# Global attention: row maxima by a scan, values two fifths at a time, the last product on GpSimd

## The chip, the cores and the metric

The kernel runs on one core of a Trainium2 chip. The time is that of one execution on the device, in microseconds (us). A core has five engines that run side by side, each through its own queue in order: TensorE (PE in the profile; its weight loads are PEld), VectorE (DVE), ScalarE (ACT), GpSimd (POOL) and SyncE (SP), which here only issues DMAs. Matmuls write to PSUM, which has eight banks of 128 x 512 fp32; VectorE and ScalarE read PSUM, GpSimd doesn't.

## The reference

Two layers of a diffusion block on 1024 latent tokens of width 1024, with 256 context tokens. Each layer has three groups of heads side by side (global attention, pooling, neighbourhood attention), each gated, and one output projection. The change touches the global attention alone: 8 query heads of 64 in two key groups, 1024 queries against 1280 keys (1024 latent, 256 context).

```python
def dense_attn(q, k, v):
    s = jnp.einsum("bqkgd,bskd->bkgqs", q, k).astype(jnp.float32)
    p = jax.nn.softmax(s, axis=-1).astype(v.dtype)
    o = jnp.einsum("bkgqs,bskd->bqkgd", p, v)
    return o.reshape(o.shape[0], o.shape[1], -1)
...
a_out = global_gqa(aq, ak, av, ak_c, av_c)
...
y = jnp.concatenate([a_out * silu(ag), b_out * silu(bg), n_out * silu(ng)], axis=-1) @ w_out[l]
```

## The kernel before

Each layer runs in stages: projections of the tokens, neighbourhood attention (with the context tokens' own attention in layer 0), global attention, output projection. TensorE's order is written out by hand (the order of the program's text); for the other engines a planner chooses the order from the program's dependencies and its own estimates of time, and once chosen it is fixed: an instruction that waits holds up all behind it on its engine.

Global attention is cut into eight **units**, gunits[0] to [7]: a unit is 512 queries (cc) of a pair of heads (hi = 0, 1) that share a key group g. A unit has these parts.

- **Maxima** (shift, L974). A softmax needs the row maxima before its exponentials. For each head, 8 matmuls of 128 queries x 512 keys (L985), each into a bank of its own with one reduction by VectorE (L986), then 2 banks of context keys (L990, L991). A last small reduction (L994) gives the negative maxima of 8 x 128 queries. shift_rows (L996) transposes them on TensorE, copies them, and two DMAs write them into row 0 of the second query operand q2, whose matmul (L1012) then adds the negative maximum and the low part of the product to the scores. The maxima of unit i are made while unit i - 1 runs: 21 steps in a list, which shift_step pops.
- **Scores** (L1006). They come transposed (keys down, queries across) in fifths kp = 0 to 4, 256 keys each. For a head and a fifth 4 matmuls (L1011, L1012) fill a tile of two banks, one exponential (L1014) reads it and writes a tile gp of 128 x 1024. There are two such tiles of banks (ps_w). s14 stands below for the scores of head 1, fifth 4.
- **Sums**: the tiles of a head are added up in gacc, fifths 1 to 3 by GpSimd (L1019, L1022), fifth 4 by VectorE (L1022), which also folds the two halves (L1024). Matmuls with ones add over the partitions (L1040).
- **Values** (L1026): for each 128 keys two matmuls of 64 output columns, one for each head, add into one bank, ps_c (L1031; the trace has two records for each such fp32 matmul). They run one fifth behind the scores; the last fifth and the sums are done in the next unit.
- **Finish** (L1037): the reciprocal of the sums by Ln, Exp and a step of refinement on VectorE (L1044 to L1048), the product of the output and the gate on GpSimd (L1049), the product of the two on VectorE (L1050), and store_u (L803), which writes the result as a high part hh on ScalarE (L806) and the rest hl on VectorE (L807), the operands of the output projection.

Maxima, transposes and sums take turns in three PSUM banks (ps_b, by ps_one); a bank is free again when its reader is done. The gp tiles and gacc share a ring of seven buffers in SBUF (tag prob, PB = 7). The loop over the units stands at L1117; unit 7 has no maxima to make.

## Time and profile before

| | us |
|---|---|
| median of 3 runs | 1550.68 (1550.53 to 1553.64) |
| the profiled execution | 1550.23 |
| its span, first to last instruction | 1548.5 |
| layer 0, global attention | from about 523 to 740 |
| layer 1, global attention | from about 1237 to 1454 |

The granted clock of TensorE was 0.989 in the mean. A row of the groups gives line, engine, operation, what it writes and reads, shape and count, then the busy time in us and the mean of one in ns, then the engine's idle time before it and who ended it. A row of the timeline gives start and length in us, then the instruction, and in brackets the idle time before it with its releaser. A row of the waits gives who waited for whom: us in total, times, the longest.

### The profile page before, as it was taken

The page shows a single profiled execution, that of the slowest core. Times are in us where ns is not written, and L with a number is a line of the kernel's source. Part 1 is how long each engine was busy: PE and PEld are TensorE (multiplying, and loading weights), DVE is VectorE, ACT ScalarE, POOL GpSimd, SP SyncE. Part 2 cuts the span into 40 slices and gives each one's busy share as a digit, 9 for nine tenths or more (in the row PEclk, how much of TensorE's full clock was granted, in tenths as well). Part 3 has the DMA queues.
Part 4 walks back from the last instruction along what each step waited for, and adds up shares of the span by engine and source line. Part 5 has one row for each costly group of instructions (what it writes and reads, how often), then busy time and mean ns, then how long its engine had stood idle before and what let it go on. Part 6 is the DMA issues. An engine that isn't in the chain of part 4 may idle for free.

```text
span 1548.5 us, 22305 instructions
## 1 busy us (share of the span) xinstructions
PE 1474.4 (95%) x8001; PEld 1074.7 (69%) x8001; DVE 855.6 (55%) x1721; ACT 661.8 (43%) x1296; POOL 506.0 (33%) x586
## 2 busy tenths in 40 slices
PE   5999999999899999998999999999989899999999
PEld 3787777788788555454788888878778754554577
DVE  3535234552477687875534444464357768786522
ACT  4543132333587544444322443332458544444400
POOL 0232336000132556566001132470013166565300
PEclk8999999999999999999999999999999999999999
DMA  9436455537746110101412223253696211001331
GB/s 306 148 98 219 128 157 164 165 103 191 169 123 167 45 42 21 41 7 41 176 55 104 87 79 104 76 149 83 174 218 158 79 31 41 22 21 41 120 132 55
DMA packets 153040, 167.91 MB, mean 108 GB/s; under 512 B 35384, under 2 KB 112032, under 8 KB 152864
## 3 DMA queue, kind: packets, MB, share of 16 engines
q1 hardware_dynamic: 152928, 166.48, 37.1%
q8 instruction: 63, 1.03, 0.3%
q14 instruction: 49, 0.40, 0.1%
HBM read 126.45 MB, written 40.86 MB: 108 GB/s over the span
## 4 chain that ended last, share of the span: by engine, by line
PE 52%; DVE 8%; ACT 3%; issue 2%; DMA 1%; POOL 1%; SPq 0%; DVEq 0%; ACTq 0%; POOLq 0%
PE ps_c L1031 7%; PE ps_w L1184 4%; PE ps_w L1187 4%; PE ps_w L1185 4%; PE ps_w L1011 4%; PE ps_w L1012 3%; PE ps_w L417 3%; PE ps_w L418 3%; PE ps_w L416 3%; PE ps_b L985 3%; DVE gt L1050 2%; DVE gmx L986 2%; PE ps_c L877 1%; DVE gacc L1022 1%; PE ps_w L426 1%
## 5 line engine op out<-in xcount | busy, mean ns | idle before, releaser
L1014 ACT ACTIVATE gp<-ps_w 128x1024 f32<-128x1024 f32 x160 | 162.4, 1022 | 183.5 <-PE ps_w L1012 147.2
L416 PE MATMUL ps_w<-wh,hh 128*128 128x512 f32 (+1 forms) x624 | 235.7, 378 | 1.7 <-ACT wh L285 1.7
L417 PE MATMUL ps_w<-wl,hh 128*128 128x512 f32 (+1 forms) x624 | 228.9, 367 | 0.3 <-DVE wl L286 0.2
L418 PE MATMUL ps_w<-wh,hl 128*128 128x512 f32 (+1 forms) x624 | 228.3, 366 | 0.0
L986 DVE TENSOR_REDUCE gmx<-ps_b 128x1 f32<-128x512 f32 x256 | 171.7, 685 | 75.7 <-PE ps_b L985 71.6
L1031 PE MATMUL ps_c<-gp,av 128*64 128x512 f32 x640 | 165.7, 611 | 10.4 <-ACT gp L1014 10.4
L1022 POOL TENSOR_TENSOR gacc<-gacc,gp 128x1024 f32<-128x1024 f32 x64 | 161.4, 2550 | 25.8 <-ACT gp L1014 25.5
L416 PEld LDWEIGHTS ps_w<-wh,hh 128*128 128x128 f32 x624 | 118.6, 190 | 26.8 <-issue 4.4
L418 PEld LDWEIGHTS ps_w<-wh,hl 128*128 128x128 f32 x624 | 117.9, 189 | 20.6
L417 PEld LDWEIGHTS ps_w<-wl,hh 128*128 128x128 f32 x624 | 118.1, 189 | 19.3 <-DVE wl L286 0.8
L1012 PE MATMUL ps_w<-gq,kst 128*128 128x512 f32 x320 | 126.2, 394 | 0.0
L1184 PE MATMUL ps_w<-woh,hh 128*128 128x512 f32 x272 | 109.1, 401 | 0.0
L1185 PE MATMUL ps_w<-wol,hh 128*128 128x512 f32 x272 | 107.1, 394 | 0.0
L637 DVE TENSOR_REDUCE qss<-sq 128x8 f32<-128x512 f32 (+2 forms) x58 | 31.1, 537 | 131.6 <-ACT sq L635 131.3
L1031 PEld LDWEIGHTS ps_c<-gp,av 128*64 128x64 f32 x640 | 42.7, 137 | 88.0 <-issue 65.7
L1019 POOL TENSOR_TENSOR gacc<-gp 128x1024 f32<-128x1024 f32 x32 | 75.8, 2368 | 50.7 <-ACT gp L1014 50.7
L286 DVE TENSOR_TENSOR wl<-wraw,wh 128x512 fp32r<-128x512 f32 (+1 forms) x96 | 66.5, 708 | 38.1 <-ACT wh L285 36.6
L1187 PE MATMUL ps_w<-woh,hl 128*128 128x512 f32 x272 | 85.0, 394 | 0.0
L852 ACT ACTIVATE prob<-ps_w,nm 128x768 f32<-128x768 f32 (+2 forms) x88 | 73.4, 834 | 21.9 <-DVE nm L841 16.6
L424 PE MATMUL ps_w<-hh,wh 128*128 128x512 f32 (+1 forms) x208 | 80.7, 388 | 0.9 <-ACT wh L285 0.9
L870 ACT ACTIVATE probt<-ps_b 128x512 f32<-128x512 f32 (+2 forms) x152 | 73.6, 532 | 17.1 <-PE ps_b L868 16.7
L635 ACT ACTIVATE sq<-ps_w 128x512 f32<-128x512 f32 (+2 forms) x58 | 27.9, 481 | 121.7 <-PE ps_w L418 121.7
(225 smaller groups left out, 2992.1 us busy)
## 6 DMA issues: line engine op xcount, KB each, us to landing
wmod<-in_w_mod_dram SPq DMA_DIRECT2D x48, 512.0 KB
wraw<-in_w_in_dram SPq DMA_DIRECT2D x64, 256.0 KB
gq<-qad SPq DMA_DIRECT2D x64, 128.0 KB
woraw<-in_w_out_dram SPq DMA_DIRECT2D x14, 512.0 KB
wraw<-in_w_in_dram SPq DMA_DIRECT2D x48, 128.0 KB
kst<-knd SPq DMA_DIRECT2D x16, 320.0 KB
qad<-qkhi SPq DMA_DIRECT2D x18, 256.0 KB
qad<-qklo SPq DMA_DIRECT2D x18, 256.0 KB
```

The lines of the kernel that those rows point to most:

```text
L416: PE.matmul(ps[:, :n], a, wh[:, off:off + n], start=(k == 0), stop=False)
L417: PE.matmul(ps[:, :n], a, wl[:, off:off + n], start=False, stop=False)
L418: PE.matmul(ps[:, :n], b, wh[:, off:off + n], start=False, stop=(k == KT - 1))
L424: PE.matmul(ps[:, :n], wh[:, fs], hh[:, k, ts_], start=(k == 0), stop=False)
L986: DVE.reduce_max(out=mx[:, qt, half:half + 1], in_=S, axis=AX.X)
L1012: PE.matmul(S[:, i, :], k2[:, kc], st.q2[hi], start=False, stop=True)
L1014: ACT.activation(out=p, in_=S, func=AF.Exp)
L1022: eng.tensor_tensor(out=st.acc[hi], in0=st.acc[hi], in1=pf, op=ALU.add)
L1031: PE.matmul(st.o[hi * 64:(hi + 1) * 64, :], av[:, kt, g * 64:(g + 1) * 64], st.p[hi, kp][:, i, :], start=(kt == 0), stop=(kt == NTT - 1))
L1184: PE.matmul(ps[:, i2, :], a, oh[:, cs], start=(k == 0), stop=False)
L1185: PE.matmul(ps[:, i2, :], a, ol[:, cs], start=False, stop=False)
L1187: PE.matmul(ps[:, i2, :], b, oh[:, i2 * 512:(i2 + 1) * 512], start=False, stop=(k == KT - 1))
```

## The change

- For units 2 to 7 shift2 takes the place of shift. The context keys' maxima come first, by the same reductions. Then, for each 128 queries, both banks of 512 keys are filled one after the other (a pair). ScalarE copies the first into SBUF, and one running scan of VectorE over the second bank and the copy, begun with the context maximum, keeps the maximum so far; its last element is the row maximum. A negation per two scans takes the place of the last reduction. The copies lie in the memory of the two tables of the neighbourhood attention, which become one tile each. Steps have weights now (a pair counts 2), and shift_step gives credits, so a unit still makes 21 of them.
- The values run two fifths at a time: after s02 fifths 0 and 1, after s04 fifths 2 and 3, and the last fifth in the next unit after s01. Right behind it stand the sums and the finish, which came after the third fifth before.
- The finish's last product moves to GpSimd, without its sign; the sign goes into the write of hh and the difference hl.
- gacc leaves the ring: it lies in the memory of nv (values of the neighbourhood attention) for even units and in two kst buffers for odd ones. In unit 7, head 0's additions from fifth 2 on go to VectorE.

```diff
--- before.py
+++ after.py
@@ -742,7 +742,8 @@
         akx, attx = ExitStack(), ExitStack()
         ak_ = akx.enter_context(pool(f"attk{l}", side=left))
 
-        tab_bufs = [(ak_.tile([P, 14, 64], F32, name=f"ntab{i}"), ak_.tile([P, 10, 64], F32, name=f"itab{i}")) for i in range(2)]
+        tab_mem = [ak_.tile([P, 24, 64], F32, name=f"tab{i}") for i in range(2)]
+        tab_bufs = [(t[:, 0:14], t[:, 14:24]) for t in tab_mem]
 
         def kst():
             return ak_.tile([P, NT], F32R, name="kst", bufs=6)
@@ -954,7 +955,7 @@
             return gks[g]
 
 
-        def ga_unit(cc, g, pr):
+        def ga_unit(n, cc, g, pr):
             f = 2 * g + pr
             cs = slice(cc * 512, (cc + 1) * 512)
             st = _Env()
@@ -986,12 +987,41 @@
                     DVE.reduce_max(out=mx[:, qt, half:half + 1], in_=S, axis=AX.X)
                     return
                 q0 = 2 * (j - 8)
-                for i in range(2):
-                    PE.matmul(S[:, i * 256:(i + 1) * 256], q1[:, (q0 + i) * P:(q0 + i + 1) * P], k1[:, SEQ:NT], start=True, stop=True)
-                DVE.reduce_max(out=mx[:, q0:q0 + 2, 2], in_=S.rearrange("p (a b) -> p a b", a=2), axis=AX.X)
+                shift_ctx(hi, q0, S, mx[:, q0:q0 + 2, 2])
                 if hi and j == 9:
                     st.nn = small.tile([P, 8], F32, tag="gnn", name="gnn")
                     DVE.tensor_reduce(out=st.nn, in_=st.mx.rearrange("p h q k -> p (h q) k"), op=ALU.max, axis=AX.X, negate=True)
+            def shift_ctx(hi, q0, S, out):
+                for i in range(2):
+                    PE.matmul(S[:, i * 256:(i + 1) * 256], st.q1[hi][:, (q0 + i) * P:(q0 + i + 1) * P], gk(g)[0][:, SEQ:NT],
+                              start=True, stop=True)
+                DVE.reduce_max(out=out, in_=S.rearrange("p (a b) -> p a b", a=2), axis=AX.X)
+            def shift2(i):
+                hi, j = divmod(i, 6)
+                if i == 0:
+                    load2()
+                    st.mx = small.tile([P, 8], F32, tag="gmx2", name="gmx2")
+                    st.nn = small.tile([P, 8], F32, tag="gnn", name="gnn")
+                if j < 2:
+                    c = 4 * hi + 2 * j
+                    shift_ctx(hi, 2 * j, ps_one("ps_m"), st.mx[:, c:c + 2])
+                    return
+                qt = j - 2
+                if qt % 2 == 0:
+                    st.run = tab_mem[qt // 2].rearrange("p a k -> p (a k)")[:, 0:1024].rearrange("p (a b) -> p a b", a=2)
+                S = [ps_one("ps_m") for _ in range(2)]
+                for half in range(2):
+                    PE.matmul(S[half], st.q1[hi][:, qt * P:(qt + 1) * P], gk(g)[0][:, half * 512:(half + 1) * 512], start=True, stop=True)
+                r, c = st.run[:, qt % 2], 4 * hi + qt
+                ACT.activation(out=r, in_=S[0], func=AF.Copy)
+                DVE.tensor_tensor_scan(out=r, data0=S[1], data1=r, initial=st.mx[:, c:c + 1], op0=ALU.max, op1=ALU.max)
+                if qt % 2:
+                    DVE.tensor_scalar(out=st.nn[:, c - 1:c + 1], in0=st.run[:, :, 511], scalar1=-1.0, scalar2=None, op0=ALU.mult)
 
             def shift_rows():
 
@@ -1015,10 +1045,10 @@
                 st.p[hi, kp] = p
                 pf = p.rearrange("p a b -> p (a b)")
                 if kp == 1:
-                    st.acc[hi] = ap_.tile([P, 1024], F32, name="gacc", tag="prob", bufs=PB)
+                    st.acc[hi] = accs[n % 2][hi]
                     POOL.tensor_tensor(out=st.acc[hi], in0=st.p[hi, 0].rearrange("p a b -> p (a b)"), in1=pf, op=ALU.add)
                 elif kp > 1:
-                    eng = DVE if kp == 4 else POOL
+                    eng = DVE if kp == 4 or (n == 7 and hi == 0) else POOL
                     eng.tensor_tensor(out=st.acc[hi], in0=st.acc[hi], in1=pf, op=ALU.add)
                 if kp == 4:
                     DVE.tensor_tensor(out=st.acc[hi][:, 0:512], in0=st.acc[hi][:, 0:512], in1=st.acc[hi][:, 512:1024], op=ALU.add)
@@ -1034,31 +1064,40 @@
                     st.osb = ap_.tile([P, 512], F32, name="gosb", tag="fin", bufs=4)
                     ACT.activation(out=st.osb, in_=st.o, func=AF.Copy)
 
+            def sums():
+                st.s = ps_one("ps_gs")
+                for hi in range(2):
+                    PE.matmul(st.s[hi * 64:(hi + 1) * 64, :], ones, st.acc[hi][:, 0:512], start=True, stop=True)
             def finish():
-                s_ps = ps_one("ps_gs")
-                for hi in range(2):
-                    PE.matmul(s_ps[hi * 64:(hi + 1) * 64, :], ones, st.acc[hi][:, 0:512], start=True, stop=True)
                 gt = ap_.tile([P, 512], F32, name="ggate", tag="fin", bufs=4)
                 SP.dma_start(out=gt, in_=agd[f, :, cs])
                 r0 = ap_.tile([P, 512], F32, name="gr0", tag="fin", bufs=4)
-                ACT.activation(out=r0, in_=s_ps, func=AF.Ln)
+                ACT.activation(out=r0, in_=st.s, func=AF.Ln)
                 ACT.activation(out=r0, in_=r0, func=AF.Exp, scale=-1.0)
                 t1 = ap_.tile([P, 512], F32, name="gt1", tag="fin", bufs=4)
-                DVE.tensor_tensor(out=t1, in0=s_ps, in1=r0, op=ALU.mult)
+                DVE.tensor_tensor(out=t1, in0=st.s, in1=r0, op=ALU.mult)
                 DVE.scalar_tensor_tensor(out=t1, in0=t1, scalar=-2.0, in1=r0, op0=ALU.add, op1=ALU.mult)
                 POOL.tensor_tensor(out=gt, in0=gt, in1=st.osb, op=ALU.mult)
-                DVE.scalar_tensor_tensor(out=t1, in0=t1, scalar=-1.0, in1=gt, op0=ALU.mult, op1=ALU.mult)
-                store_u(f, cc * 512, 512, t1)
-
-            return shift, scores, values, finish, load, shift_rows
-
-        gunits = [ga_unit(cc, g, pr) for cc in range(2) for g in range(2) for pr in range(2)]
+                POOL.tensor_tensor(out=gt, in0=gt, in1=t1, op=ALU.mult)
+                hi, lo = hh[:, f, cs], hl[:, f, cs]
+                ACT.activation(out=hi, in_=gt, func=AF.Identity, scale=-1.0)
+                DVE.scalar_tensor_tensor(out=lo, in0=gt, scalar=-1.0, in1=hi.bitcast(F32), op0=ALU.mult, op1=ALU.subtract)
+            return shift, scores, values, finish, load, shift_rows, shift2, sums
+        gunits = [ga_unit(4 * cc + 2 * g + pr, cc, g, pr) for cc in range(2) for g in range(2) for pr in range(2)]
 
         shifts = []
         for i, u in enumerate(gunits):
-            own = [lambda u=u, j=j: u[0](j) for j in range(20)]
-            shifts += own[:2] + ([gunits[i - 1][5]] if i else []) + own[2:]
-        shifts.append(gunits[-1][5])
+            if i < 2:
+                own = [(1, lambda u=u, j=j: u[0](j)) for j in range(20)]
+            else:
+                own = [(1 if j % 6 < 2 else 2, lambda u=u, j=j: u[6](j)) for j in range(12)]
+            shifts += own[:2] + ([(1, gunits[i - 1][5])] if i else []) + own[2:]
+        shifts.append((1, gunits[-1][5]))
         for i in range(2):
             early(len(units) - 12, gunits[i][4])
 
@@ -1077,10 +1116,16 @@
         n_shifts = 7 if last else 10
         n_ahead = 21 + GA_AHEAD
 
+        credit = [0]
         def shift_step(n, least=0):
-            for _ in range(n):
-                if len(shifts) > least:
-                    shifts.pop(0)()
+            credit[0] += n
+            while len(shifts) > least and shifts[0][0] <= credit[0]:
+                w, fn = shifts.pop(0)
+                credit[0] -= w
+                fn()
+            if len(shifts) <= least:
+                credit[0] = 0
 
         n_all = len(shifts)
         for n, u in enumerate(units + [None, None]):
@@ -1114,29 +1159,31 @@
             split_w(wo[0], raw, slice(i * 512, (i + 1) * 512))
 
         nu = len(gunits)
+        nvf = nv.rearrange("p t c -> p (t c)")
+        accs = [[nvf[:, 0:1024], nvf[:, 1024:2048]],
+                [ak_.tile([P, NT], F32, name="gacc", tag="kst", bufs=6)[:, 0:1024] for _ in range(2)]]
         for i in range(nu):
-            _, scores, values, finish, _, _ = gunits[i]
+            _, scores, values, finish = gunits[i][:4]
             pv = gunits[i - 1] if i else None
             if i + 2 < nu:
                 gunits[i + 2][4]()
             for kp in range(5):
-                lagv = None
-                if kp:
-                    lagv = lambda h, kp=kp: values(kp - 1, h)
-                elif pv:
-                    lagv = lambda h: pv[2](4, h)
                 scores(0, kp)
                 shift_step(1)
-                if lagv:
-                    lagv(0)
-                    lagv(1)
+                if kp == 1 and pv:
+                    pv[2](4, 0)
+                    pv[2](4, 1)
+                    pv[7]()
+                    pv[3]()
+                elif kp in (2, 4):
+                    for j in range(4):
+                        values(kp - 2 + j // 2, j % 2)
                 shift_step(2 if kp == 4 else 1)
                 scores(1, kp)
                 shift_step(2)
-                if kp == 2 and pv:
-                    pv[3]()
-        gunits[-1][2](4, 0)
-        gunits[-1][2](4, 1)
+        for fn in (lambda: gunits[-1][2](4, 0), lambda: gunits[-1][2](4, 1), gunits[-1][7]):
+            fn()
         akx.close()
         lay.close()
```

## The prediction

> **What bounds the kernel now.** I read the page first, then the busy times by stretch of time around the global attention of each layer, then one unit of it on TensorE and VectorE, and last the waits.
>
> ```profile
> span 1548.5 us, 22305 instructions
> PE 1474.4 (95%) x8001; PEld 1074.7 (69%) x8001; DVE 855.6 (55%) x1721; ACT 661.8 (43%) x1296; POOL 506.0 (33%) x586
> 519.00:740.00 221.00, 207.71 (x861) 108.23 (x861) 157.32 (x206) 101.26 (x125) 129.93 (x61) 0.99 0.09 29
> 1233.00:1455.00 222.00, 210.45 (x900) 110.54 (x897) 159.90 (x207) 99.80 (x119) 129.53 (x58) 0.99 0.11 32
> 587.70:614.83 27.13, 25.89 (x111) 13.76 (x113) 21.53 (x30) 12.63 (x16) 16.33 (x8) 1.00 0.10 30
> 681.40:708.16 26.76, 24.83 (x103) 12.60 (x102) 19.27 (x24) 11.50 (x14) 15.88 (x7) 1.00 0.14 49
> 708.16:739.99 31.83, 28.40 (x97) 12.31 (x96) 14.96 (x12) 13.56 (x16) 16.27 (x8) 0.95 0.08 25
> 1422.60:1454.43 31.83, 28.42 (x97) 12.02 (x95) 14.96 (x12) 13.58 (x16) 16.27 (x8) 0.95 0.03 10
> ```
>
> The columns are length, then busy PE, PEld, DVE, ACT, POOL, the granted clock, DMA. TensorE is busy 95% of the whole. The change touches only the two stretches of some 221 us, where TensorE is idle 13.3 and 11.6 us. The third window is one steady unit (they repeat every 27.13 us), then come unit 6 and unit 7 of layer 0, and unit 7 of layer 1. Unit 7 has no maxima left to make and still takes 31.83. The waits say why:
>
> ```profile
> PE ps_b L985 <- DVE gmx L986: 13.7, 13, 1.2
> PE ps_c L1031 <- ACT gp L1014: 10.4, 6, 3.1
> 726.83 2.65 DVE L1050 SCALAR_TENSOR_TENSOR gt<-gt,ggate 128x512 f32<-128x512 f32 x1
> 729.51 0.63 ACT L806 ACTIVATE hh<-gt 128x512 fp32r<-128x512 f32 x1 [5.15 <-DVE gt L1050]
> 731.11 2.86 PE L1031 MATMUL ps_c<-gp,av 128*64 128x512 f32 x6 [3.14 <-ACT gp L1014]
> 733.90 0.80 PE L1011 MATMUL ps_w<-hl,kst 128*128 128x512 f32 x1
> ```
>
> Of these waits 13 are for a bank held by a maximum, about one of 1.25 per steady unit. In unit 7 ScalarE stands 5.15 us in its queue at the write L806, because L1050 took 2.65; the exponentials behind it come late, TensorE idles 3.14 and its next matmuls run slower.
>
> **The change on TensorE.** Maxima and values keep every matmul. What goes is switching:
>
> ```profile
> 589.66 0.40 PE L985 MATMUL ps_b<-kst,hh 128*128 128x512 f32 x1
> 589.99 1.94 PE L1031 MATMUL ps_c<-gp,av 128*64 128x512 f32 x8
> 591.86 0.50 PE L985 MATMUL ps_b<-kst,hh 128*128 128x512 f32 x1
> 592.20 0.40 PE L1011 MATMUL ps_w<-hl,kst 128*128 128x512 f32 x1
> 592.43 0.40 PE L1012 MATMUL ps_w<-gq,kst 128*128 128x512 f32 x1
> 599.72 0.51 PE L985 MATMUL ps_b<-kst,hh 128*128 128x512 f32 x1 [1.25 <-DVE gmx L986]
> 614.76 1.08 PE L1040 MATMUL ps_b<-gacc,ones 128*64 128x512 f32 x4
> 615.77 0.50 PE L1011 MATMUL ps_w<-hh,kst 128*128 128x512 f32 x1
> ```
>
> One 128-column matmul follows another after 0.23; into a 64-column group the step is 0.33, out of it 0.34. A group thus costs 0.2 beside its work. There were six per unit (five of values, one of sums); now there are three (last fifth with sums, two fifths, two fifths). That is 3 x 0.2 = 0.6 less, and a steady unit's busy time becomes 25.89 - 0.6 = 25.3. Without a wait that would be the unit.
>
> **The change on the other engines.**
>
> ```profile
> L986 DVE TENSOR_REDUCE gmx<-ps_b 128x1 f32<-128x512 f32 x256 | 171.7, 685 | 75.7 <-PE ps_b L985 71.6
> L1022 DVE TENSOR_TENSOR gacc<-gacc,gp 128x1024 f32<-128x1024 f32 x32 | 46.2, 1444 | 8.6 <-ACT gp L1014 8.6
> L1242 DVE TENSOR_TENSOR yg<-ps_w,gateb 128x1024 f32<-128x1024 f32 x17 | 20.8, 1222 | 76.8 <-PE ps_w L1187 76.6
> L1047 DVE TENSOR_TENSOR gt<-ps_b,gr 128x512 f32<-128x512 f32 x16 | 10.9, 684 | 26.1 <-ACT gr L1045 26.1
> L1050 DVE SCALAR_TENSOR_TENSOR gt<-gt,ggate 128x512 f32<-128x512 f32 x16 | 33.4, 2085 | 0.6
> L1035 ACT ACTIVATE gosb<-ps_c 128x512 f32<-128x512 f32 x16 | 9.6, 598 | 19.1 <-PE ps_c L1031 14.0 <-PE ps_b L1040 4.0 <-DMA ggate<-agd 1.1
> L1014 ACT ACTIVATE gp<-ps_w 128x1024 f32<-128x1024 f32 x160 | 162.4, 1022 | 183.5 <-PE ps_w L1012 147.2 <-POOL gacc L1019 35.5 <-PE ps_b L985 0.6
> L1049 POOL TENSOR_TENSOR ggate<-ggate,gosb 128x512 f32<-128x512 f32 x16 | 20.7, 1291 | 99.3 <-ACT gosb L1035 99.3
> L1022 POOL TENSOR_TENSOR gacc<-gacc,gp 128x1024 f32<-128x1024 f32 x64 | 161.4, 2550 | 25.8 <-ACT gp L1014 25.5 <-ACT gmr L1001 0.3
> 593.00 2.14 DVE L1050 SCALAR_TENSOR_TENSOR gt<-gt,ggate 128x512 f32<-128x512 f32 x1
> 595.06 1.28 DVE L986 TENSOR_REDUCE gmx<-ps_b 128x1 f32<-128x512 f32 x2
> L841 DVE TENSOR_SCALAR nm<-m 128x1 f32<-128x1 f32 x88 | 13.0, 148 | 1.1
> L1019 POOL TENSOR_TENSOR gacc<-gp 128x1024 f32<-128x1024 f32 x32 | 75.8, 2368 | 50.7 <-ACT gp L1014 50.7
> 597.85 1.21 DVE L1022 TENSOR_TENSOR gacc<-gacc,gp 128x1024 f32<-128x1024 f32 x1
> 598.98 0.68 DVE L986 TENSOR_REDUCE gmx<-ps_b 128x1 f32<-128x512 f32 x1
> 599.58 0.68 DVE L1024 TENSOR_TENSOR gacc<-gacc 128x512 f32<-128x512 f32 x1
> ```
>
> *The scan* is in no row. Two reductions in a row take 1.28 (a 0.60 step). From below a scan of 512 costs like one pass over 512 (0.68, L986 and L1047), from above like one over 1024 (1.22, L1242). I take the upper row, with the 1.13 step that L1022 shows before L986: each element passes two maxima in sequence before the next can start, so it resembles 1024 single steps more than 512. VectorE then gains almost nothing from the maxima: per unit 8 scans for 16 reductions, 9.0 for 9.6, and four negations of 0.15 for one small reduction.
>
> [...]
>
> *ScalarE* gains 8 copies of 0.60, 4.8 us: 12.6 becomes 17.4 of some 27. Where no values stand between scores, a step on TensorE is 0.92 of scores and 0.46 of a pair, on ScalarE an exponential (0.92 step) and a copy (about 0.55): 1.47 against 1.38, over four steps at most 0.4 behind, which the second score buffer covers.
>
> *The result.* L1050 (2.09 in the mean) leaves VectorE, a multiplication of 1.29 comes to GpSimd (16.33 becomes 17.6). The hh write and the last difference stay. The 2 accumulators leave the seven-buffer ring, so exponentials stop waiting for L1019 (35.5 us in L1014's row); TensorE did not wait then, so I count nothing. The gate load is issued one kp earlier and the other DMAs stay; SP's queue is nearly empty here (30 GB/s in the steady unit), so that is free. Loads of w_out into the memory of nv must now wait for unit 6's sums, early in unit 7; the output projection wants them over 15 us later. Merging the two tables into one tile costs nothing if slices are kept apart, as they must be for hh, of which other slices are loaded and written in the same stage.
>
> **New waits, in one steady unit.** A pair holds two of three banks until copy and scan are done. The copy waits in ScalarE's queue behind an exponential, the scan in VectorE's queue behind other work. I walked the order with the steps above; s is scores, P a pair, c a context step, and credits give s00 P s10 c c s01 V P s11 P s02 V P s12 P s03 c c s13 row s04 P V P s14 P.
>
> (a) From s14's start: last P at 0.92; exponential 1.13 to 2.15; copy to 2.75. If the fifth's addition (1.13) and fold (0.60) of L1022 and L1024 go first on VectorE, the scan ends at 5.1, and the first c, due at 3.9 with its reduction's bank, waits 1.3. If the scan goes first, 0.2. I cannot see the order, and take 0.75.
>
> (b) The sums' bank is held until L1047, after Ln and Exp: 2.85 after the sums' start, and the second P wants it at 2.4: 0.45.
>
> (c) The row transpose, 4.36 after the values block, needs the scan of the pair issued at 1.48: copy behind the exponential to 3.25, scan to 4.43, negation to 4.6, bank handed over: 0.35.
>
> Unit: 25.3 + 0.75 + 0.45 + 0.35 = 26.85, a gain of 0.28 x 5 units = 1.4. Unit 6 (26.76, busy 24.83): there the row comes right after s03, 2.87 instead of 4.36, and waits 1.8; 24.83 - 0.6 + 0.75 + 0.45 + 1.8 = 27.2, a loss of 0.4. Unit 0: two groups fewer, 0.4, rounded up to 0.5 for its small waits.
>
> Unit 7: 40 matmuls of scores (9.2), 40 + 4 records of 0.234 for values and sums (10.3), the fifth and sums of unit 6 (2.8), switching 0.7: 23.0. Waits: three scores in a row run at the exponential's pace twice (0.3 + 0.3), the last exponential before the last fifth 1.2, others 0.3: 25.1 against 31.83, a gain of 6.7. The hh write then stands behind a GpSimd product and is free 4 to 6.5 us after the sums, while the first exponential after s02's is due 7 us after them: the values block of 3.7 us covers it. If that cover is gone, the gain shrinks to some 2.
>
> Per layer 1.4 - 0.4 + 0.5 + 6.7 = 8.2; for two 16.4. The profiled execution took 1550.2 (its span 1548.5), the median of the runs is 1550.7. 1550.2 - 16.4 = **1534**.
>
> **Rivals.**
>
> *A cheap scan* (step 0.60): (a) 0.35 in the middle, (c) nothing, the row in unit 6 1.2. Unit 26.1, unit 6 26.2: 5 x 1.03 + 0.55 + 0.5 + 6.7 = 12.9 per layer, 1524. For it: L1047 reads PSUM and SBUF at 0.68. Against: two chained maxima. Chance 0.20.
>
> *No new waits at all*: unit 25.3, unit 6 24.2: 9.2 + 2.5 + 0.5 + 6.7 = 18.9 per layer, 1512. It needs both a cheap scan and the friendly order. 0.10.
>
> *No change*: the hh write still holds up exponentials in unit 7 (gain 2), and (a) is 1.3: 0.5 + 2 - 1.4 - 0.9 = 0.2 per layer, 1550. 0.12.
>
> *Slower: GpSimd's queue.* VectorE's last addition L1022 needs GpSimd's. GpSimd starts after s01's exponential, 5.8 into the unit, has 2 x 2.37 + 4 x 2.55 + 2 x 1.29 = 17.5 to do and about 1.6 of waits for exponentials on the way, so it ends at 24.9; VectorE wants it at 27.6 (2.15 after s14's start): 2.7 spare. L1050's 2.14 beside a GpSimd addition, where one pass is 0.68, shows that products of two SBUF operands hold each other up; four such on VectorE are left (0.68 x 3 + 1.21 = 3.2 us). If all collide, the spare is gone, and scans stand behind the waiting L1022. At 2 us past the spare the unit is 28.85: 5 x -1.72 - 2.4 + 0.5 + 6.7 = -3.8 per layer, 1558. It decides from 1.4 us past it on (8.2 / 6 units). 0.15. [...]
>
> **How the numbers follow.** Forecast 1534 (own range 1528 to 1540 by (a)): 0.43; 1524: 0.20; 1512: 0.10; 1550: 0.12; 1558: 0.15. The range 1515 to 1555 leaves out most of the slow case and half of the best. A difference under 0.2% (3 us) can't be told from none: faster 0.73, same 0.12, slower 0.15.
>
> **What would show it.** Scan rows near 1.2 or 0.68; three groups per unit of 64 columns; unit 7 near 25 without a wait over 1.5; the longest new waits at L990's successor for the scan and at the row transpose. Wrong if steady units are over 27.13 (then look at GpSimd's additions), or if unit 7 keeps a wait for L1014 behind the hh write.

## The result and the profile after

| | before | after |
|---|---|---|
| median, us | 1551.99 (1550.53 to 1553.64, 4 runs) | 1578.74 (1577.69 to 1579.5, 4 runs) |
| ratio to before, 95% interval | | 1.0176 (1.0164 to 1.0188) |
| span of the profiled execution | 1548.5 | 1577.7 |
| global attention, layer 0 and 1 | 217.1, 217.0 | 225.4, 223.6 |
| output projection, layer 0 and 1 | 115.2, 77.9 | 122.3, 83.7 |
| a steady unit (1 to 5) | 27.13 | 29.2 |
| unit 6, layer 0 and 1 | 26.70, 26.71 | 29.98, 28.38 |
| unit 7, layer 0 and 1 | 31.83, 31.84 | 26.10, 26.08 |

The kernel became 1.8% slower; the forecast was 1% faster. (A unit's length is from its first score matmul to that of the next; the output projection's is from its first matmul to its last.) Of the 29.2 us between the spans 15.0 stand in global attention, 12.9 in the output projections, where the forecast had counted the late loads of w_out as nothing, and 1.3 in the rest.

The page of after, and the busy times by stretch: both stretches of global attention, a stretch as long as one steady unit, and unit 7 of layer 0. The columns are length, PE, PEld, DVE, ACT, POOL, granted clock, DMA.

```profile
PE 1472.3 (93%) x8001; PEld 1073.9 (68%) x8001; DVE 864.4 (55%) x1649; ACT 712.1 (45%) x1392; POOL 507.2 (32%) x598
521.30:746.71 225.41, 201.95 (x841) 105.85 (x840) 160.68 (x165) 124.28 (x165) 129.30 (x63) 0.99 0.10 31
1253.79:1477.40 223.61, 200.16 (x840) 105.21 (x838) 162.23 (x166) 123.96 (x165) 129.04 (x62) 1.00 0.10 30
632.19:661.40 29.21, 26.03 (x110) 13.80 (x109) 22.33 (x24) 16.73 (x24) 16.67 (x8) 1.00 0.10 28
720.62:746.71 26.09, 24.53 (x97) 10.54 (x96) 15.28 (x11) 13.80 (x16) 14.56 (x7) 1.00 0.26 91
```

TensorE has the same matmuls as before, but in a steady unit it is now idle 3.2 us instead of 1.2. VectorE, at 22.3 of 29.2, has no more to do per unit of time than before. The groups and the waits of after:

```profile
L1022 DVE TENSOR_TENSOR_SCAN tab<-ps_b,gmx,tab 128x512 f32<-128x512 f32 x96 | 122.6, 1277 | 51.6 <-ACT tab L1021 51.6
L1021 ACT ACTIVATE tab<-ps_b 128x512 f32<-128x512 f32 x96 | 57.0, 594 | 48.7 <-PE ps_b L1019 47.6
PE ps_b L1019 <- DVE gt L1079: 18.0, 12, 1.5
PE ps_b L1029 <- DVE gnn L1024: 10.9, 12, 2.2
PE ps_b L998 <- DVE tab L1022: 10.5, 12, 0.9
PE ps_w L1231 <- ACT woh L285: 5.6, 2, 2.8
```

The scan takes 1.28. Three waits come once in each of the 12 units that make maxima for a later one by scans: 1.5 at the sums' bank, 0.9 at the row transpose, 0.9 at the context step. Together they are 3.3 us per unit in the mean. In a steady unit they are 3.0, as the row transpose waits 0.66 there and 2.2 in unit 6. The waits that the change was to remove (L985 for a maximum, 13.7 us; L1031 for an exponential, 10.4 us) are down to 1.1 and 2.7. The timeline shows how the two largest kinds arise:

```profile
631.48 0.66 DVE L1054 TENSOR_TENSOR gacc<-gacc 128x512 f32<-128x512 f32 x1
632.06 1.27 DVE L1022 TENSOR_TENSOR_SCAN tab<-ps_b,gmx,tab 128x512 f32<-128x512 f32 x1
632.49 0.59 ACT L1021 ACTIVATE tab<-ps_b 128x512 f32<-128x512 f32 x1
633.45 1.22 DVE L1052 TENSOR_TENSOR gacc<-gacc,gp 128x1024 f32<-128x1024 f32 x1
634.59 1.28 DVE L1022 TENSOR_TENSOR_SCAN tab<-ps_b,gmx,tab 128x512 f32<-128x512 f32 x1
635.92 0.74 PE L998 MATMUL ps_b<-kst,hl 128*128 128x256 f32 x4 [0.88 <-DVE tab L1022]
...
639.28 1.03 PE L1070 MATMUL ps_b<-gacc,ones 128*64 128x512 f32 x4
640.36 0.60 ACT L1076 ACTIVATE gr<-ps_b 128x512 f32<-128x512 f32 x1 [0.26 <-PE ps_b L1070]
640.85 0.59 ACT L1021 ACTIVATE tab<-ps_b 128x512 f32<-128x512 f32 x1
641.33 0.63 ACT L1077 ACTIVATE gr<-gr 128x512 f32<-128x512 f32 x1
641.48 1.28 DVE L1022 TENSOR_TENSOR_SCAN tab<-ps_b,gmx,tab 128x512 f32<-128x512 f32 x1 [2.58 <-ACT tab L1021]
642.68 0.67 DVE L1079 TENSOR_TENSOR gt<-ps_b,gr 128x512 f32<-128x512 f32 x1
643.40 0.72 PE L1019 MATMUL ps_b<-kst,hl 128*128 128x512 f32 x2 [1.48 <-DVE gt L1079]
```

The copy at 632.49 is done at 633.1, but its scan begins only at 634.59, behind an earlier scan and an addition; the context step waits for the scan's bank until 635.92. Below, the sums have their bank from 639.28 on. A pair's copy stands between Ln and Exp on ScalarE, and its scan in front of L1079 on VectorE, so the bank is free at 643.35, 4 us after the sums began, and the next pair waits 1.48.

The output projection of layer 0 begins at 746.71:

```profile
749.68 1.26 POOL L1083 TENSOR_TENSOR ggate<-ggate,gt 128x512 f32<-128x512 f32 x1 [2.11 <-DVE gt L1080]
750.97 0.63 ACT L1085 ACTIVATE hh<-ggate 128x512 fp32r<-128x512 f32 x1 [2.89 <-POOL ggate L1083]
751.50 2.94 ACT L285 ACTIVATE woh<-woraw 128x1024 fp32r<-128x1024 f32 x3
752.60 0.50 PE L1231 MATMUL ps_w<-woh,hh 128*128 128x512 f32 x1 [2.81 <-ACT woh L285]
753.86 0.50 PE L1232 MATMUL ps_w<-wol,hh 128*128 128x512 f32 x1 [0.76 <-DVE wol L286]
754.20:757.90 3.70, 3.70 (x11) 2.88 (x10) 1.87 (x2) 0.95 (x2) 0.00 (x0) 0.54 0.77 209
```

ScalarE waits 2.89 us with the last hh write, and the three weight splits L285 stand behind it. TensorE waits 2.81 and 0.76 for them, and then (last row, a stretch of 3.7 us) runs at a granted clock of 0.54. Layer 1 shows the same: waits of 2.82 and 0.77, and a granted clock of 0.54 from 1484.60 to 1488.30.

### The profile page after: what moved, and what is told of

Same layout as the page of the kernel before. It is cut to its first block, busy times and chain, and to the rows that moved or that the text cites. A ratio compares the mean times of both kernels' runs of the same rounds, so it can differ in the third digit from the quotient of the medians.

```text
span 1577.7 us, 22394 instructions
## 1 busy us (share of the span) xinstructions
PE 1472.3 (93%) x8001; PEld 1073.9 (68%) x8001; DVE 864.4 (55%) x1649; ACT 712.1 (45%) x1392; POOL 507.2 (32%) x598
## 4 chain that ended last, share of the span: by engine, by line
PE 43%; DVE 8%; issue 6%; ACT 5%; DMA 3%; POOL 1%; SPq 1%; POOLq 0%; DVEq 0%; ACTq 0%
PE ps_c L1061 6%; PE ps_w L1232 4%; PE ps_w L1231 4%; PE ps_w L1234 4%; DVE tab L1022 4%; PE ps_w L417 3%; PE ps_w L418 3%; PE ps_w L416 3%; PE ps_w L1041 2%; PE ps_w L1042 2%; ACT gp L1044 2%; PE ps_c L878 1%; PE ps_b L1019 1%; PE ps_b L1070 1%; ACT prob L853 1%
## 5 line engine op out<-in xcount | busy, mean ns | idle before, releaser
L1044 ACT ACTIVATE gp<-ps_w 128x1024 f32<-128x1024 f32 x160 | 163.1, 1024 | 85.1 <-PE ps_w L1042 84.7
L1061 PE MATMUL ps_c<-gp,av 128*64 128x512 f32 x640 | 150.9, 603 | 0.2
L1022 DVE TENSOR_TENSOR_SCAN tab<-ps_b,gmx,tab 128x512 f32<-128x512 f32 x96 | 122.6, 1277 | 51.6 <-ACT tab L1021 51.6
L1061 PEld LDWEIGHTS ps_c<-gp,av 128*64 128x64 f32 x640 | 42.2, 137 | 84.5 <-issue 82.5
L426 PE MATMUL ps_w<-hh,wl 128*128 128x512 f32 (+1 forms) x208 | 79.3, 381 | 0.0
L1052 POOL TENSOR_TENSOR nv<-nv,gp 128x1024 f32<-128x1024 f32 x32 | 75.2, 2380 | 12.2 <-ACT gp L1044 12.2
```

What stands on the lines that cost most here:

```text
L1022: DVE.tensor_tensor_scan(out=r, data0=S[1], data1=r, initial=st.mx[:, c:c + 1], op0=ALU.max, op1=ALU.max)
L1044: ACT.activation(out=p, in_=S, func=AF.Exp)
L1061: PE.matmul(st.o[hi * 64:(hi + 1) * 64, :], av[:, kt, g * 64:(g + 1) * 64], st.p[hi, kp][:, i, :], start=(kt == 0), stop=(kt == NTT - 1))
```

## The experiments

Two questions were open. For global attention: is it the pair of copy and scan (T1), the early sums that hold their bank (T2), or VectorE held up beside GpSimd (T3)? For the output projection: GpSimd's late product (P1), or the place of the accumulators, with its late loads of w_out (P2)?

**First four: one part undone or moved in the changed kernel.** `noscan`: the old maxima in all units.

```diff
-            if i < 2:
+            if i < 8:
                 own = [(1, lambda u=u, j=j: u[0](j)) for j in range(20)]
```

> Units 2 to 7 make their maxima by reductions again; the rest of the change stays. The steady unit took 27.13 us before and 29.25 after. If the pair of copy and scan is the cause (T1), the unit is the one before less three groups of 64 columns (3 x 0.34): 26.1, at most 27.1, and the kernel about 1550. If the early sums that hold their bank are the cause (T2), the wait of some 1.5 at the sums' bank stays: 27.6 to 28.5, about 1566. If it is VectorE held up beside GpSimd (T3), 28.5 or more. The output projection stays 13 us longer than before in any case.

A steady unit and the wait at the sums' bank:

```profile
627.39:654.73 27.34, 25.93 (x111) 13.77 (x110) 21.60 (x29) 12.88 (x16) 17.14 (x8) 1.00 0.10 30
PE ps_b L986 <- DVE gt L1079: 6.0, 12, 0.5
```

Steady units 27.34, global attention 211.6 and 211.8, output projections 120.9 and 84.4, kernel 1551.3, ratio 0.9994 (0.9983 to 1.0004). The scan costs 1.9 us a unit. The unit lies between the forecasts of T1 and T2, as the wait at the sums' bank is 0.5 now. Global attention is over 5 us per layer shorter than before the change, and the output projection gives all of it back.

`vals1`: values one fifth at a time, sums and finish after the third fifth.

```diff
-                if kp == 1 and pv:
-                    pv[2](4, 0)
-                    pv[2](4, 1)
-                    pv[7]()
-                    pv[3]()
-                elif kp in (2, 4):
-                    for j in range(4):
-                        values(kp - 2 + j // 2, j % 2)
+                if kp:
+                    values(kp - 1, 0)
+                    values(kp - 1, 1)
+                elif pv:
+                    pv[2](4, 0)
+                    pv[2](4, 1)
...
+                if kp == 2 and pv:
+                    pv[7]()
+                    pv[3]()
```

> Values one fifth at a time, sums and finish after the third fifth, as before; the scan, the product on GpSimd and the accumulators' places stay. T2 (the early sums): the wait of 1.5 at the sums' bank goes, three groups of 64 columns come back (1.0): a steady unit of 28.2 to 28.8, and the kernel about 1570. T1 (copy and scan): the waits stay and the groups are added, 29.5 to 30.3, the kernel 1580 or more.

Units of 29.8, kernel 1585.8, ratio 1.0211 (1.0189 to 1.0233). As T1 has it: the wait at L1079 is gone, and waits for the scan (L1019 for L1022, 14.7 us in 12) and for exponentials (L1061 for L1044, 12.6 us) stand in its place. Beside the 27.13 of before, which has the same order, scan, product and accumulators cost 2.7 a unit. Unit 7 took 28.0.

`sumscopy`: the sums' bank copied out first.

```diff
-                ACT.activation(out=r0, in_=st.s, func=AF.Ln)
+                sc = ap_.tile([P, 512], F32, name="gsc", tag="fin", bufs=4)
+                ACT.activation(out=sc, in_=st.s, func=AF.Copy)
+                ACT.activation(out=r0, in_=sc, func=AF.Ln)
...
-                DVE.tensor_tensor(out=t1, in0=st.s, in1=r0, op=ALU.mult)
+                DVE.tensor_tensor(out=t1, in0=sc, in1=r0, op=ALU.mult)
```

> ScalarE copies the sums' bank into SBUF at once, and the logarithm and the first refinement read the copy: the bank is free after one copy in place of Ln, Exp and a multiplication. T2: the wait at that bank falls from 1.5 to about 0.3 and the steady unit to about 28.0. T1: the copy is 0.6 more on ScalarE, in front of the copies of the pairs, and the unit stays at 29.2 or grows. In this kernel the first weight split of the output projection stands ahead of the last hh write on ScalarE: if that order costs the output projection its 13 us (P1), it loses 3 to 7 us per layer of them; if the late loads of w_out do (P2), nothing.

Worse, at 1590.5, ratio 1.0244 (1.0224 to 1.0264), units 29.8 to 30.6 (29.8 and 30.2 in the two where the granted clock stayed at 1.00). The wait for L1079 is gone, and one for the pair's copy has come:

```profile
PE ps_b L1019 <- ACT tab L1021: 32.5, 12, 2.7
```

The pair's copy stands behind one more instruction on ScalarE. The output projections fell to 119.5 and 80.9, by 2.8 each, which is just short of the 3 to 7 that P1 gave; P2 gave nothing.

`prod7`: in the last unit the product on VectorE.

```diff
+                if n == 7:
+                    DVE.scalar_tensor_tensor(out=t1, in0=t1, scalar=-1.0, in1=gt, op0=ALU.mult, op1=ALU.mult)
+                    store_u(f, cc * 512, 512, t1)
+                    return
                 POOL.tensor_tensor(out=gt, in0=gt, in1=t1, op=ALU.mult)
```

> In the last unit alone the product of output and gate goes back to VectorE, with the write of hh as before; global attention stays as it is, and the loads of w_out stay late. P1 (the hh write, late behind GpSimd's product, stands ahead of the weight splits in ScalarE's queue): the first split goes ahead of it again, the output projections take about 116 and 78.5 us in place of 122.3 and 83.7, and the kernel 1566 to 1569. P2 (late loads of w_out): no change, 1578.

1569.7, ratio 1.0109 (1.0092 to 1.0126); output projections 118.4 and 79.8, three fifths of the way back, and the low clock is gone (1.00 from 748.00 to 752.00, behind the wait). One split stands ahead of the hh write now; the other part of that split, on VectorE, comes behind the product, and TensorE waits 1.5 for it in each layer. So P1 isn't the whole.

**Second four.** `relu` keeps the pair, but its second half takes one pass. The maximum of two numbers is one of them plus the positive part of their difference; that difference TensorE can make, from a difference of the keys.

```diff
-                    PE.matmul(S[half], st.q1[hi][:, qt * P:(qt + 1) * P], gk(g)[0][:, half * 512:(half + 1) * 512], start=True, stop=True)
+                    PE.matmul(S[half], st.q1[hi][:, qt * P:(qt + 1) * P], gk(g)[0][:, 512:1024] if half else kd[0], start=True, stop=True)
-                ACT.activation(out=r, in_=S[0], func=AF.Copy)
-                DVE.tensor_tensor_scan(out=r, data0=S[1], data1=r, initial=st.mx[:, c:c + 1], op0=ALU.max, op1=ALU.max)
+                ACT.activation(out=r, in_=S[0], func=AF.Relu)
+                DVE.tensor_tensor_reduce(out=r, in0=S[1], in1=r, scale=1.0, scalar=st.mx[:, c:c + 1], op0=ALU.add, op1=ALU.max,
+                                         accum_out=st.m[:, c:c + 1])
```

> The pair stays, but its second half takes one pass: the first bank gets the queries' product with the difference of the two halves of the keys, ScalarE writes its positive part, and VectorE adds the second bank and takes the maximum in one instruction (that form takes 759 ns for 128 x 512 in the profile of before, the scan 1277). The differences of the keys are three passes per layer. Nothing else changes. If the length of the scan is what costs (T1a), VectorE has 4 us less per unit, the banks are held 0.5 shorter, and the steady unit falls from 29.25 to 27.0 to 27.6, the kernel to about 1557. If it is the copy that waits in ScalarE's queue while the pair holds two of three banks (T1b), the unit stays at 28.5 to 29.2 and the kernel over 1570.

1579.1, ratio 1.0184 (1.0168 to 1.0199): no clear answer. Units 1, 3 and 5 took 27.5 to 27.6, as T1a had it; units 2 and 4 took 29.4 to 32.6, since the key differences took a buffer of the queries' ring, and TensorE waited up to 2.7 us for them (in the longest the granted clock was 0.90 besides). It was repeated with a buffer of its own (below).

`ring67`: the accumulators of units 6 and 7 in the ring.

```diff
-                    st.acc[hi] = accs[n % 2][hi]
+                    st.acc[hi] = accs[n % 2][hi] if n < 6 else ap_.tile([P, 1024], F32, name="gacc", tag="prob", bufs=PB)
```

> The accumulators of units 6 and 7 alone lie in the ring of seven again, so the memory that w_out is loaded into is free earlier by the planner's reckoning; on ScalarE three weight splits then stand ahead of the last hh write, as before the change. The last product stays on GpSimd. P2 (the place of the accumulators sets the order): the output projections go back to 115 to 117 and 78 to 79, the kernel to 1565 to 1567. P1 alone (GpSimd's product as such): at least half of the 13 us stays, 1572 or more. Units 6 and 7 may grow by up to 1 each for buffers of the ring.

Output projections 116.7 and 78.0, kernel 1569.3, ratio 1.0119 (1.0103 to 1.0135). Of the 12.9 us 11.3 are back, though GpSimd still makes the product; P2 holds. The timeline of this run at the same place:

```profile
746.50 0.60 ACT L1076 ACTIVATE gr<-ps_b 128x512 f32<-128x512 f32 x1 [0.60 <-PE ps_b L1070]
747.00 1.05 ACT L285 ACTIVATE woh<-woraw 128x1024 fp32r<-128x1024 f32 x1
747.94 0.62 ACT L1077 ACTIVATE gr<-gr 128x512 f32<-128x512 f32 x1
748.46 1.99 ACT L285 ACTIVATE woh<-woraw 128x1024 fp32r<-128x1024 f32 x2
753.95 0.63 ACT L1085 ACTIVATE hh<-ggate 128x512 fp32r<-128x512 f32 x1 [3.49 <-POOL ggate L1083]
```

The hh write comes later than in the changed kernel, with a longer wait, and does no harm, as three splits stand ahead of it. Unit 7 grew from 26.1 to 28.3, more than expected, and returned 4.4 us of the gain. Some 1.6 of each 2.2 is the clock: TensorE waited 1.8 there for an exponential, and the granted clock over the unit was 0.94 in both layers.

`noscan_ring` has both edits, reductions and the ring.

> Maxima by reductions again and the accumulators of units 6 and 7 in the ring; values two fifths at a time, the early finish and the product on GpSimd stay. If the two losses are separate and add up, global attention takes 211.7 in each layer as with reductions alone and the output projections 115 to 117 and 78 to 79: 1551.3 - 11.5, about 1540, faster than before by 0.7%. If they are one, 1548 or more.

1542.5, ratio 0.9948 (0.9932 to 0.9963); global attention 214.1 and 212.4, output projections 115.2 and 77.9. The two losses are separate and add up. Unit 7 took 28.3 and 26.7, with the same wait of 1.9 for an exponential in both layers, but a granted clock of 0.94 in layer 0 and of 1.00 in layer 1.

`noscan_ring_dve` has the product on VectorE in all units besides.

```diff
-                POOL.tensor_tensor(out=gt, in0=gt, in1=t1, op=ALU.mult)
-                hi, lo = hh[:, f, cs], hl[:, f, cs]
-                ACT.activation(out=hi, in_=gt, func=AF.Identity, scale=-1.0)
-                DVE.scalar_tensor_tensor(out=lo, in0=gt, scalar=-1.0, in1=hi.bitcast(F32), op0=ALU.mult, op1=ALU.subtract)
+                DVE.scalar_tensor_tensor(out=t1, in0=t1, scalar=-1.0, in1=gt, op0=ALU.mult, op1=ALU.mult)
+                store_u(f, cc * 512, 512, t1)
```

> As the run above, but with the product of output and gate on VectorE and the write of hh as before, in all units. It tells what shortens the last unit (31.83 before, 26.0 with the change). If it is the product's move to GpSimd, the last unit goes back to 29 to 31 and the steady one grows to 27.6 or more. If it is the order of values and finish (the hh write covered by a block of values), the last unit stays at 26 to 27 and the kernel at about 1540.

**1536.3, ratio 0.9905 (0.9889 to 0.9922)**: faster than both kernels. Global attention 210.0 in each layer. Its waits, a steady unit and unit 7 of layer 0:

```profile
PE ps_b L986 <- DVE gmx L987: 13.3, 13, 1.1
PE ps_b L986 <- DVE gt L1079: 6.1, 12, 0.5
PE ps_b L986 <- DVE gmx L1000: 5.5, 12, 0.5
626.69:654.03 27.34, 25.41 (x111) 13.76 (x109) 23.68 (x30) 12.84 (x15) 16.36 (x7) 1.00 0.10 29
706.57:731.61 25.04, 24.28 (x97) 10.54 (x96) 18.01 (x14) 13.67 (x16) 12.43 (x6) 1.00 0.12 37
```

Unit 7 is at 25.0 with the product on VectorE: the product's move to GpSimd is not what shortens it. The steady unit is 27.34, not below the 27.13 of before, though TensorE's busy time fell from 25.89 to 25.41: the waits for banks grew, from 1.05 a unit (13.7 in 13) to 2.0 (the three rows).

**Three on the scan.** `relu2` repeats `relu` with a buffer for the key differences, made once. To make room, one accumulator moves into the memory of one table, and the pairs' copies keep to the other; those lines are not shown.

```diff
+                    if n == 2:
+                        kd.append(ak_.tile([P, NT], F32R, name="kd", tag="kst", bufs=6))
+                        for g2 in (1, 0):
+                            k1 = gk(g2)[0].bitcast(F32)
+                            DVE.tensor_tensor(out=kd[0][:, g2 * 512:(g2 + 1) * 512], in0=k1[:, 0:512], in1=k1[:, 512:1024], op=ALU.subtract)
```

> As the earlier run with one pass in place of the scan, but the differences of the keys have a buffer of their own, made once for both key groups, so that no unit waits for a buffer of the queries. All the rest of the change stays. If the scan's length costs 1.7 per unit, as the undisturbed units of that run had it (27.55 for 29.25), all ten steady units are now 27.4 to 27.7, and the kernel 1561 to 1564. If those units were short only because their neighbours were long, the mean stays at 28.5 or more.

1558.7, ratio 1.0046 (1.0031 to 1.0062); units 1 to 5 take 27.46 to 27.57 in both layers. The instruction that takes the scan's place, the waits and a steady unit:

```profile
L1030 DVE CUSTOM_DVE_ANT_0 tab<-ps_b,tab,gmx 128x512 f32<-128x512 f32 x96 | 71.7, 747 | 68.4 <-ACT tab L1029 68.4
PE ps_b L1038 <- DVE gnn L1033: 12.3, 12, 2.4
PE ps_b L1025 <- DVE gt L1088: 12.0, 12, 1.0
629.54:657.10 27.56, 25.69 (x111) 13.87 (x109) 17.84 (x32) 16.80 (x24) 17.00 (x8) 1.00 0.10 30
```

747 ns in place of 1277 in the same chain takes 1.7 of the unit's 1.9 us away. Copies and pairs as such cost 0.2 beside reductions, and about 1.1 in unit 6 (27.04 in layer 1, beside 25.95 in `noscan`); in layer 0 unit 6 took 28.66, at a granted clock of 0.94. The wait at the context step is gone, that at the sums' bank is 1.0 in place of 1.5.

`relu2_ring_dve` has it with the ring and the product on VectorE.

> One pass in place of the scan, the product on VectorE and the accumulators of units 6 and 7 in the ring. The last unit 25.0 and the output projections 115.3 and 77.9, as with reductions; only the maxima differ from that run (1536.3). If VectorE's load per unit sets the unit, it has about 3 us less than with reductions and the steady unit falls under 27.3: 1528 to 1535. If what is left is the pair's hold on two of three banks, the unit is 27.5 or more, unit 6 over 26, and the kernel 1537 to 1543.

1543.9, ratio 0.9954 (0.9938 to 0.9970). Units of 27.3 to 27.4 and a unit 6 of 26.95 and 28.55 (at granted clocks of 1.00 and 0.94): not better than reductions. VectorE's load of 19.4 against 23.7 per unit buys nothing.

`scan_ring_dve` is the fastest version with the scan, that is without the line of `noscan`.

> The scan with all else as in the fastest run so far (product on VectorE, accumulators of units 6 and 7 in the ring, values two fifths at a time). If the scan's loss is its own, the steady unit is 29.2 to 29.5, the last unit 25.0, and the kernel 1536.3 + 10 x 1.9 + 2 x 3 = 1558 to 1563. If a good part of it comes from GpSimd's second product, which holds up VectorE (an addition of 3.30 and a refinement of 2.67 in the profile of the change), the unit falls to 28.5 or less and the kernel under 1551.

1563.8, ratio 1.0079 (1.0055 to 1.0104); steady units 29.2, unit 7 25.1, and the waits are those of the change almost to the number:

```profile
PE ps_b L1019 <- DVE gt L1079: 17.9, 12, 1.5
PE ps_b L1029 <- DVE gnn L1024: 11.0, 12, 2.3
PE ps_b L998 <- DVE tab L1022: 10.4, 12, 0.9
```

So GpSimd's second product has no part in the 29.2. T3 had missed already, as it gave 28.5 or more for `noscan` and 27.34 came. VectorE is still held up beside GpSimd's additions here (L1080 takes 2.25 in the mean); what that adds to the scans' wait no run parts off.

**Three on the order.** `late_sums` moves sums and finish alone.

```diff
-                    pv[7]()
-                    pv[3]()
...
                 scores(1, kp)
                 shift_step(2)
+                if kp == 2 and pv:
+                    pv[7]()
+                    pv[3]()
```

> The change with one thing moved: the sums and the finish stand after the third fifth of the next unit, as before, while the last fifth's values stay after the second. If the early sums cause the wait of 1.5 at their bank by themselves (T2), the steady unit loses it and gains one more switch to 64 columns and back (0.34): 28.0 to 28.2. If the scan's chain is the cause and the sums only the place where it shows (T1), another wait takes its place, and the unit is 29.0 to 29.8.

1588.5, ratio 1.0247 (1.0231 to 1.0264), units 30.9 to 31.7, worse than either theory had it. The wait for L1079 is replaced by one for the scan (the granted clock in the unit shown was 0.94, but the first steady unit of layer 1 took 30.9 at 1.00 too):

```profile
PE ps_b L1019 <- DVE tab L1022: 33.8, 12, 3.2
637.11:668.06 30.95, 26.98 (x111) 14.96 (x110) 22.37 (x24) 16.66 (x24) 18.09 (x8) 0.94 0.08 26
```

T2 falls: the early sums are where the scan's wait shows, not its cause.

`nrd_late` has the same edit on the fastest version.

> The fastest version so far (reductions, product on VectorE, accumulators of units 6 and 7 in the ring) with the sums and the finish after the third fifth as before; the values stay two fifths at a time. It parts what shortens the last unit (31.83 before, 25.0 there). If it is the early finish, the hh write comes late again and the last unit is 29 to 31.5; if it is the longer blocks of values, it stays under 26.5. The steady unit: 27.2 to 27.5, as the wait of 0.5 at the sums' bank goes and a switch of 0.34 comes.

1547.2, ratio 0.9974 (0.9964 to 0.9983): unit 7 at 26.0 and 26.1, steady units 28.1 to 29.0 (the long ones at a granted clock of 0.94), for 25.0 and 27.36 with the early finish. The steady part came out 0.6 or more longer than expected: TensorE waits 1.4 a unit for maxima (18.1 us in 13), not 1.0.

`nrd_pool7` leaves head 0's additions of unit 7 on GpSimd.

```diff
-                    eng = DVE if kp == 4 or (n == 7 and hi == 0) else POOL
+                    eng = DVE if kp == 4 else POOL
```

> The fastest version so far, with the additions of head 0 in the last unit on GpSimd as in all others. If these additions on VectorE are what shortens the last unit, it is 28 or more; if not, 25 to 26, with at most 1 more at the start of the output projection for later sums.

1541.3, ratio 0.9940 (0.9924 to 0.9957), unit 7 at 27.8: the additions on VectorE are worth 2.7 there. 1.7 of it is a wait of the sums (L1070) for the fold of the accumulator.

## Why the prediction was wrong

The profiled execution was to lose 16.4 us and gained 29.2, which is 45.6 off. By its own terms:

| step | forecast, us | measured, us | off, both layers |
|---|---|---|---|
| steady unit | 26.85 | 29.23 | 10 x 2.38 = 23.8 |
| unit 6 | 27.2 | 29.98, 28.38 | 4.0 |
| unit 7 | 25.1 | 26.10, 26.08 | 2.0 |
| unit 0, change | -0.5 | +0.25, +0.29 | 1.5 |
| w_out loads, output projection | 0 | +7.1, +5.8 | 12.9 |
| the rest of the kernel | 0 | +1.3 | 1.3 |

**The scan itself was sized right.** The upper row (1.22, a 1.13 step) was taken, and it measured 1.277, which is 1.86 times the 0.685 of a reduction of the same 512 elements (L986 before the change). The reason that I had given, two maxima in sequence, no run tests; the runs show the length alone.

**The new waits (a), (b), (c) were mis-sized**: 0.75 + 0.45 + 0.35 = 1.55 forecast, 0.88 + 1.48 + 0.66 = 3.0 measured in the steady unit shown; (b) is most of the miss. Another 0.7 stands in TensorE's busy time, 26.03 for a forecast of 25.3. Busy time is not work alone: with reductions it is 25.93 (`noscan`) and 25.41 (`noscan_ring_dve`) for the same matmuls in units of the same 27.34, so short waits are counted in it. The places were the right ones, and each was worked out as if the pair were alone in the queues. In (b) I let the sums' bank go after Ln, Exp and the multiplication in a row, 2.85 after the start; the trace has a copy between Ln and Exp and a scan ahead of the multiplication, which makes it 4.1. In (a) I took the mean of two orders; the trace shows the scan behind an addition and another scan, nearer the bad end, and the same lag reaches the row transpose in (c). `relu2` shows that these terms hang on the scan's length: 0.53 less per scan is 1.7 less per unit.

In unit 6 the row transpose waited 2.24 and 2.25, for 1.8 in the forecast, and in layer 0 the clock added to it. The stretches are unit 6 of layer 0 and of layer 1:

```profile
690.63:720.61 29.98, 25.27 (x100) 12.77 (x99) 19.03 (x20) 15.22 (x21) 16.65 (x8) 0.94 0.03 9
1422.94:1451.33 28.39, 23.65 (x101) 12.21 (x100) 19.78 (x20) 15.07 (x21) 16.66 (x8) 1.00 0.03 10
```

The matmuls and the waits are the same; the 1.6 between the two is the low granted clock behind the transpose's wait. Of unit 6's 4.0 in the table that is 1.6, which the forecast had no term for. In unit 0 the switching was saved (busy time of 21.96 for 22.71), but its end waits 1.18 for the first scan.

**The load did not decide.** Per unit VectorE is busy 21.6 with reductions (23.7 with the product on it too), 22.3 with scans and 17.8 with one pass; the units take 27.34 (both), 29.2 and 27.56. What a pair changes, as I read it, is how long two of three banks are held: two matmuls, a copy of 0.59, a scan of 1.28, and the queues in front of both. A reduction holds one bank for 0.68. The scan's length was varied with the pair kept (`relu2`); the number of banks was not varied by itself.

**The saving in switching came and was lost again.** 25.3 of busy time was forecast for a steady unit and 25.41 came in `noscan_ring_dve`; yet the unit is 27.34, as waits for banks took it back. The forecast kept the old waits at nothing, where the old wait of 1.05 for a maximum stays with reductions and other waits join it.

**Unit 7 was nearly right in size (25.1 forecast, 26.1 measured), in part by luck, and its reason was partly wrong.** The working had 23.0 of matmuls and 2.1 of waits; the trace has 24.5 of busy time and waits of 1.3, two misses that partly cancel. I had the values block cover the hh write behind GpSimd's product. The hh write is covered but for a wait of 1.2 per layer, and the product's place is not the cause: with it on VectorE the unit takes 25.0. With the finish late as before and the long values blocks kept, it takes 26.0 (`nrd_late`), so the blocks, with head 0's additions on VectorE, give 5.8 of the 6.8 us between 31.83 and 25.0, and the early finish 1.0. Some 1.6 of the 5.8 is the low clock that unit 7 had before (a granted clock of 0.95 over the 31.83 us). The additions are worth 2.7 in the fastest version, a term that I had not priced. The blocks are worth 2.1 in the changed kernel: `vals1`, without them, has a unit 7 of 28.0, and `late_sums`, with them, one of 25.9, both with the late finish. That 25.9 also says that in the changed kernel the early finish gained nothing in unit 7.

**The loads of w_out were costed at nothing** because they would land 15 us ahead of their use. That was true on the chip (the first two are issued at 730.2 and 730.6, their traffic is over by 736, and TensorE stands still for their split from 749.8 on), and beside the point: with the accumulators in that memory the planner put the last hh write ahead of the splits on ScalarE. `ring67` shows that the place sets this order; that the planner expected the loads later is my reading, as its estimates are not on record. The order is fixed, so the splits waited for GpSimd's product. I had named that product only as a danger inside unit 7. `ring67` gives 11.3 of the 12.9 us back with the product unmoved; `prod7` gives 7.8 with the memory unmoved. It takes both parts of the change to make the whole loss.

**The rival that ended slower** had the sign and not the mechanism: GpSimd's queue as the bound, VectorE waiting for its additions. Such waits exist, here just ahead of the lines shown first:

```profile
627.06 3.30 DVE L1052 TENSOR_TENSOR gacc<-gacc,gp 128x1024 f32<-128x1024 f32 x1 [1.83 <-POOL gacc L1052]
630.29 1.27 DVE L1022 TENSOR_TENSOR_SCAN tab<-ps_b,gmx,tab 128x512 f32<-128x512 f32 x1
```

VectorE waited 1.83 us for GpSimd, and its addition then took 3.30, both ahead of a scan. But a GpSimd with less to do (15.4 us per unit, `scan_ring_dve`) left the unit at 29.2. How much of the queueing ahead of the scans the additions of both engines make was not tried.

## What to carry to other kernels

A new instruction between a full bank and its release is priced by the whole time that the bank is held, queues in front of each reader included (4.1 us for the sums' bank here, where 2.85 was forecast), and, as I read it, by how many banks are held at once; an engine's busy time can fall while the unit grows (from reductions in `noscan` to one pass in `relu2`, VectorE's from 21.6 to 17.8, the unit from 27.34 to 27.56). Where a planner orders the engines, a buffer moved into other memory can change the order of instructions far away, so look at the next stage too: which instruction with a late input now stands ahead of one that the next stage needs. And take a bundle apart: here two of its parts, the longer blocks of values and the early finish, with one engine's help in the last unit, are worth 0.95%, and its other three (the scan, the product on GpSimd, the accumulators' place in the last units) hid it.

## What the runs showed of the hardware

- After waits of 2.81 and 0.76 us within 4 us TensorE's granted clock was 0.54 over the next 3.7 us; a single wait of 1.5 at the same place in `prod7` left it at 1.00 (748.00 to 752.00). Single waits of about 2 us went either way: after 2.24 in unit 6 of the change the clock over the unit was 0.94 in layer 0, after 2.25 in layer 1 it was 1.00. What decides between the two these runs don't show.
- Of the 7.1 us that layer 0's output projection lost, the two waits are 3.6 and the slow stretch some 3.7 x 0.46 = 1.7. The other 1.8 is not explained; `ring67`, which has neither, keeps 1.5 of it (116.7 for 115.2).
- The refinement L1080 took 0.69 us in the last unit of `prod7` and 2.16 in the mean of the change; a VectorE addition of 1.22 took 3.30 beside one of GpSimd's. Which instruction is held up depends on the order: L1080 takes 0.68 in the mean of `noscan`, and with the product on VectorE that product, L1083, takes 2.11 with reductions (`noscan_ring_dve`) and 0.94 with scans (`scan_ring_dve`), where L1080 takes 2.25.
- An addition with a running maximum in one instruction took 747 ns for 128 x 512 (`relu2`), where the scan took 1277.
